# Layer 0's values: half of the columns by seven block products instead of eight, with raw weights kept in the scores' memory, and the instruction order set by a written table of rank changes

## The chip, the cores and the metric

The program runs on one core of a Trainium2 chip. The metric is device time in microseconds of one execution. Five engines matter: TensorE (PE in the profile; its weight loads are PEld), VectorE (DVE), ScalarE (ACT), GpSimd (POOL) and SyncE (SP), which here only issues DMA transfers.

## The reference, cut to what matters

A two-layer encoder over 512 tokens of width 1024, float32 throughout. Layer 0 mixes tokens with neighbourhood attention (16 heads of 64, an 8 x 64 grid of tokens, a window of 16 columns), layer 1 with three dilated windowed attentions that are merged. Each is followed by an output projection and a SwiGLU feed-forward of width 2816, with an RMS norm before and after.

```python
def neighbourhood_attention(x, w_qkv, w_o, rpb):
    qkv = (x @ w_qkv).reshape(b, rows, GRID_W, 3, N_HEADS, HEAD_DIM)
    ...                                   # scores + bias, masked softmax p, for each grid row
        return jnp.einsum('bhqrk,bhrkd->bhqd', p.astype(vr.dtype), vr)
    ...
    return o @ w_o

def reference(...):
    for layer in range(DEPTH):
        h = rms_norm(x, norm_mix_pre[layer])
        h = neighbourhood_attention(...) if layer % 2 == 0 else dilated_attention(...)
        x = x + rms_norm(h, norm_mix_post[layer])
        h = rms_norm(x, norm_ffn_pre[layer])
        x = x + rms_norm(swiglu(h, ...), norm_ffn_post[layer])
```

The change touches `x @ w_qkv` of layer 0 for the V columns 512 to 1023, and the order in which all instructions of the program are issued.

## The kernel before, in words

**Arithmetic.** A float32 product is done as three fast matmuls. `split` writes a high part h (ACT, L437) and a low part l = value - h (DVE, L438) of each operand, and `mm3` issues h·h, h·l, l·h (L449, L450, L451), each normally 128x256. Small products of the attentions use plain float32 matmuls that fill only half of the 128x128 array, two side by side: P·V of layer 0 (`window_pv`, L845), and in layer 1 the second scores (L1350) and P·V (L1419, L1425).

**Seven products.** The large weight products are cut into 2x2 blocks and done with seven block products instead of eight, with sums of blocks on both sides. For activations the sums are built once in the pre-norm (`operands`, transposes `tr_a` at L671, sums on POOL at L695 to L701). For weights, class `Seven` and its subclass `Values` do it: `p1`, `p2`, `sums`, `d1`, `s2`, `s4`, `sums2`, `s3`, `x2b`; POOL adds raw weight blocks (in `Values` L577, L579, L580, L585), ACT and DVE split the sums, the sinks combine the results. Layer 0's query and key columns (`qk_unit`, banks `pp_n`), both feed-forwards and layer 1 work so. Layer 0's values do not: `v_quarter` makes 256 columns at a time, with 8 x 4 x 3 = 96 matmuls of 128x256 (banks `vp_n`), four quarters in all (`vq`).

**Layer 0 in stages.** Pre-norm, four quarters of V, then for each of eight pairs of heads: the pair's query and key unit, the scores `s` (L794, L795, L805, L806), maximum on DVE (`tensor_tensor_reduce`, profile lines L813, L817), exponent on ACT (L820), scaling by the reciprocal on ACT (L1213) and POOL (L1215), transposes `ta`, `tb` (L827 to L834), P·V `o` (L845). Then the output projection `yo`, residual and norm (`tr_o`), gate and up (`gu`), down (`yd`). Layer 1 goes on with `vp_d`/`vd`, `pp_d`, `sa`, `sb`, `t`, `o`, `yo`, and its feed-forward. Raw weights arrive by SP's queue (L433, `load2`) in a ring of two buffers, `raw`.

**Order.** Code order does not set what an engine does next. Class `Order` collects all instructions with their dependences, plans them with a list scheduler (`run`: among the ready instructions of an engine, lowest rank first) and fixes the resulting order of each engine's queue (`pin`). Every engine is in-order afterwards: a waiting instruction holds everything behind it. Before, `pin` makes 20 orders by planning forward and backward in turn, rates each by `usual` (three runs of a noisy model, `through`), takes the best and then tries, for each 100 us piece, the ranks of the others.

Of the kernel before, what the change touches and what calls it, by code (L numbers as in the profile page):

```python
# [78 lines left out]
def _cost(i, e):  # L79
# [49 lines left out]
    return 100, 100, False, 0, 0  # L129


class Order:
# [150 lines left out]
    def through(self, order, costs):  # L283

        left, ready, at, last = [len(p) for p in self.pred], [0.0] * len(self.all), [0] * 5, 0.0
        free, locked, half, kind, pipe = [0.0] * 5, [0.0] * 5, [0.0] * 2, 0, 0.0
        rest = [e for e in range(5) if order[e]]
        while rest:
            now, e, k = min((max(free[e], ready[order[e][at[e]]]), e, order[e][at[e]]) for e in rest
                            if not left[order[e][at[e]]])  # L290
            taken, later, lock, mode, size = costs[k]
            s = max(now, pipe - AHEAD) if e == 4 else max(now, locked[5 - e]) if lock else now
            if e == 0:
                if mode > 2:
                    s = max(s + SWITCH.get((kind, 3), 0), half[mode - 3])
                    half[mode - 3] = s + later - 200
                else:
                    s = max(s + SWITCH.get((kind, mode), 0), max(half) + 95)
                    taken += 100 * (kind == 3)
                kind = min(mode, 3)  # L300
            if lock:
                locked[e] = s + taken
            if size:
                pipe = max(s + taken, pipe) + size / RATE
                end = pipe + LANDING + later
            else:
                end = s + later
            free[e], last = s + taken, max(last, end)
            for v in self.succ[k]:
                same = self.engine[v] == e and not size  # L310
                ready[v] = max(ready[v], s + taken if same and e == 0 else end if same else end + SYNC)
                left[v] -= 1
            at[e] += 1
            if at[e] == len(order[e]):
                rest.remove(e)
        return last

    def usual(self, order):

        ends = []  # L320
        for seed in range(3):
            r, costs = random.Random(seed), []
            for e, (taken, later, lock, mode, size) in zip(self.engine, self.costs):
                if size:
                    later = r.gauss(300, 700) if size < 4e5 else r.gauss(50, 800)
                    later *= 1.6 if e == 3 else 1
                else:
                    later += r.expovariate(1 / 15)
                costs.append((taken, later, lock, mode, size))
            ends.append(self.through(order, costs))  # L330
        return sum(ends) / len(ends)

    def pin(self, tc, times, span):
        rank, found = list(range(len(self.all))), []

        self.costs = [(t, LATE if 0 < size < 2e4 else later, lock, mode, size) for t, later, lock, mode, size in self.costs]
        for _ in range(times):
            starts, order, end = self.run(rank, False)
            found.append((self.usual(order), end, rank, starts, order))
            starts, _, end = self.run([-s - c[1] for s, c in zip(starts, self.costs)], True)  # L340
            rank = [end - s - c[0] for s, c in zip(starts, self.costs)]
        found.sort(key=lambda f: f[0])

        best, end, rank, base, order = found[0]
        for lo in np.arange(0.0, max(base), span):
            part = [k for k, s in enumerate(base) if lo <= s < lo + span]
            for _, _, other, _, _ in found[1:13]:
                mixed, shift = list(rank), float(np.median([rank[k] - other[k] for k in part]))
                for k in part:
                    mixed[k] = other[k] + shift  # L350
                _, new, e = self.run(mixed, False)
                usual = self.usual(new) if e < end + 3000 else best
                if usual < best:
                    best, end, rank, order = usual, e, mixed, new
        for q in order:
            for m, n in zip(q, q[1:]):
                tc.add_manual_dep(self.all[n], self.all[m].name,
                                  mybir.DependencyInfo(mybir.DependencyClass.NoSync, mybir.DependencyReason.DATA),
                                  reason="order")
# [3 lines left out]
def encoder_kernel(ctx: ExitStack, tc: tile.TileContext, a: dict, out: bass.AP):  # L363
# [20 lines left out]
    def bank(use, name):  # L384
        return tagged(psum, [P, 512], F32, use, name, BANKS[use])
# [701 lines left out]
    def hl(mem, i, n):  # L1087
        return mem[:, i * D:i * D + n], mem[:, i * D + n:i * D + 2 * n]
# [81 lines left out]
    def whole(v):  # L1170
# [12 lines left out]
                    raw0 if qd == 0 else None) for qd in range(4)]  # L1183
# [8 lines left out]

    for j in range(PAIRS):
# [323 lines left out]
    order.pin(tc, 20, 1e5)  # L1517
# [82 lines left out]
```

## Time and profile before

| what | value |
|---|---|
| median of 3 runs | 1460.94 us (1460.33 to 1461.76) |
| profiled execution | 1460.49 us, of which the span is 1458.7 us |
| PE busy | 1423.1 us (98%), 10788 matmul records |
| DVE, ACT, POOL busy | 1179.3 us (81%), 902.1 us (62%), 541.0 us (37%) |
| mean granted TensorE clock | 0.997 |
| chain that ended last | PE 82%, DVE 7%, ACT 5%, issue 2%, DMA 1%, POOL 1% |

The span is the profiled stretch; the execution's own time lies 1.8 us above it. A plain float32 matmul shows as two records, since it runs in two passes; that is why the trace has about 400 more matmuls than the program. In the timeline, records of one line that follow each other are shown as one row with a count (x8).

### The profile page before, as it was taken

To read this page: it belongs to the slowest core of one execution; us is meant where nothing else is said; L and a number is where in the kernel's file an instruction comes from. 1 tells how busy PE (TensorE), PEld (TensorE's weight loads), DVE (VectorE), ACT (ScalarE), POOL (GpSimd) and SP (SyncE) were. 2 spreads that over 40 slices of the span, in tenths; PEclk is the share of its full clock that TensorE was granted. 3 is DMA by queue.
4 is the path that set the end of the run, shared out by engine and by line. 5 is a ranking of instruction groups with operands and counts; after the bars stand their busy time and mean duration, and the time that the engine had idled before them with its cause. 6 is when DMAs were issued, how large, how long until landed. Compare 5 with 4: busy or idle time off the path is not lost.

```text
span 1458.7 us, 27918 instructions
## 1 busy us (share of the span) xinstructions
PE 1423.1 (98%) x10788; PEld 1318.6 (90%) x10788; DVE 1179.3 (81%) x1876; ACT 902.1 (62%) x1819; POOL 541.0 (37%) x398
## 2 busy tenths in 40 slices
PE   7999999999999999999999999999999999999997
PEld 6998877999999888999999999999877999999886
DVE  5499976899999888878678678787667989998877
ACT  4478873655555657544477677887775645555664
POOL 5345524544430001765553433344213644340001
PEclk9999999999999999999999999999999999999999
DMA  5356578788234674445433343343675788944662
GB/s 204 125 196 166 186 249 215 257 240 219 99 117 142 198 231 164 156 154 173 131 105 102 111 139 95 97 146 117 218 222 201 212 213 259 269 151 152 200 218 95
DMA packets 86645, 253.22 MB, mean 174 GB/s; under 512 B 19312, under 2 KB 31600, under 8 KB 84464
## 3 DMA queue, kind: packets, MB, share of 16 engines
q1 hardware_dynamic: 77696, 197.69, 41.0%
q0 software_dynamic: 8672, 53.48, 14.3%
q8 instruction: 85, 1.39, 0.4%
q14 instruction: 48, 0.39, 0.1%
q10 hardware_dynamic: 144, 0.26, 0.0%
HBM read 229.24 MB, written 68.29 MB: 204 GB/s over the span
## 4 chain that ended last, share of the span: by engine, by line
PE 82%; DVE 7%; ACT 5%; issue 2%; DMA 1%; POOL 1%; SPq 0%; POOLq 0%; DVEq 0%; ACTq 0%
PE gu L449 9%; PE gu L450 9%; PE gu L451 9%; PE pp_d L449 4%; PE pp_d L450 4%; PE pp_d L451 4%; PE yd_s L451 3%; PE yd_s L449 3%; PE yd_s L450 3%; PE vd L449 2%; PE vd L450 2%; PE vd L451 2%; PE yd_pp L451 2%; PE yd_pp L449 2%; PE yd_pp L450 2%
## 5 line engine op out<-in xcount | busy, mean ns | idle before, releaser
L657 POOL TENSOR_TENSOR rs_yd<-v_yd,mhalf 128x1 f32<-128x1 f32 x8 | 13.2, 1654 | 259.0 <-DVE v_yd L655 259.0
L450 PE MATMUL gu<-rxc,h_a 128*128 128x256 f32 x352 | 98.9, 281 | 1.3 <-DVE rxc L674 1.3
L449 PE MATMUL gu<-rxc,h_a 128*128 128x256 f32 x352 | 98.4, 280 | 1.0 <-ACT h_a L437 0.7
L449 PE MATMUL gu<-rxa,h_c 128*128 128x256 f32 x352 | 98.6, 280 | 0.6 <-DVE mem L915 0.4
L451 PE MATMUL gu<-rxc,l_a 128*128 128x256 f32 x352 | 98.6, 280 | 0.1
L449 PE MATMUL gu<-rxa,h_b 128*128 128x256 f32 x352 | 97.9, 278 | 0.1
L451 PE MATMUL gu<-rxa,l_b 128*128 128x256 f32 x352 | 97.7, 278 | 0.2 <-DVE l_b L438 0.2
L450 PE MATMUL gu<-rxa,h_b 128*128 128x256 f32 x352 | 97.8, 278 | 0.0
L450 PE MATMUL gu<-rxa,h_c 128*128 128x256 f32 x352 | 97.6, 278 | 0.0
L451 PE MATMUL gu<-rxa,l_c 128*128 128x256 f32 x352 | 97.4, 278 | 0.0
L517 POOL TENSOR_TENSOR r_d<-r_d 128x512 f32<-128x512 f32 x24 | 35.2, 1465 | 163.3 <-DVE l_ad L438 131.3
L437 ACT ACTIVATE rxc<-mem 128x512 fp32r<-128x512 f32 (+2 forms) x90 | 55.7, 623 | 60.7 <-PE yd_pp L450 32.0
L517 POOL TENSOR_TENSOR r_gu<-r_gu 128x512 f32<-128x512 f32 x20 | 33.3, 1666 | 153.0 <-DVE l_a L438 79.4
L438 DVE TENSOR_TENSOR rxc<-mem,rxc 128x512 fp32r<-128x512 f32 (+2 forms) x90 | 64.9, 727 | 16.8 <-ACT rxc L437 16.6
L517 POOL TENSOR_TENSOR raw<-raw 128x512 f32<-128x512 f32 x24 | 40.7, 1696 | 76.2 <-DVE l_a L438 73.5
L450 PEld LDWEIGHTS gu<-rxc,h_a 128*128 128x128 f32 x352 | 66.9, 190 | 1.7 <-DVE rxc L674 1.7
L449 PEld LDWEIGHTS gu<-rxc,h_a 128*128 128x128 f32 x352 | 66.8, 190 | 1.5 <-ACT h_a L437 1.0
L449 PEld LDWEIGHTS gu<-rxa,h_c 128*128 128x128 f32 x352 | 66.2, 188 | 1.6 <-DVE mem L915 0.6
L451 PEld LDWEIGHTS gu<-rxc,l_a 128*128 128x128 f32 x352 | 66.8, 190 | 0.3 <-DVE l_a L438 0.3
L449 PEld LDWEIGHTS gu<-rxa,h_b 128*128 128x128 f32 x352 | 66.3, 188 | 0.4 <-ACT h_b L437 0.3
L451 PEld LDWEIGHTS gu<-rxa,l_b 128*128 128x128 f32 x352 | 66.2, 188 | 0.4 <-DVE l_b L438 0.4
L450 PEld LDWEIGHTS gu<-rxa,h_b 128*128 128x128 f32 x352 | 66.2, 188 | 0.3 <-DVE rxa L674 0.2
(609 smaller groups left out, 6114.2 us busy)
## 6 DMA issues: line engine op xcount, KB each, us to landing
wsum<-wd POOLq DMA_DIRECT2D x24, 1408.0 KB, 11.9
r_d<-dil_qk SPq DMA_DIRECT2D x48, 512.0 KB, 4.0
raw<-wg SPq DMA_DIRECT2D x24, 512.0 KB, 5.0
raw<-wu SPq DMA_DIRECT2D x24, 512.0 KB, 7.0
wsum<-wsum POOLq DMA_DIRECT2D x8, 1408.0 KB, 10.5
raw<-wsum SPq DMA_DIRECT2D x22, 512.0 KB, 4.3
r_gu<-wg SPq DMA_DIRECT2D x20, 512.0 KB, 4.8
r_gu<-wu SPq DMA_DIRECT2D x20, 512.0 KB, 5.6
```

What stands on the lines that cost most here:

```text
L437: act.activation(h, src, AF.Copy)
L438: dve.tensor_sub(l, src, h.bitcast(F32))
L449: i = pe.matmul(o, s[0], m[0], start=start, stop=False, skip_group_check=True)
L450: pe.matmul(o, s[0], m[1], start=False, stop=False, skip_group_check=True)
L451: pe.matmul(o, s[1], m[0], start=False, stop=stop, skip_group_check=True)
L517: self.added = e[0].tensor_add(q[0], q[0], q[2])
L657: pool.tensor_tensor(r, v, mhalf, op=ALU.pow)
```

## The change: what it does

**V.** Quarters 0 and 1 stay as they were. Quarters 2 and 3 become one `v_unit` named `nv` with the seven products, 7 x 24 = 168 matmuls of 128x256 instead of 2 x 96 = 192. Its raw weights do not use the ring `raw`: they lie in `ap[1152:3200]` and `ap[3712:5760]`, where the score buffers `p_` and `pt_` live later and where the pre-norm's buffers (`ea`) lived before; the kept product `p5` lies between them at `ap[3200:3712]`. The unit runs ahead of the loop over pairs. Over the whole program PE has 24 instructions less, POOL 4 more (the sums of raw weights, 128x1024 each), DVE 6 more and ACT 3 more. The number of transfers stays.

**Order.** `through`, `usual` and the mixing are gone. `pin` still makes the 20 orders, takes the one numbered `FIRST`, changes its ranks by a table of 83 rows (each takes a range of instructions, of one engine or of all, and shifts their rank or takes it from another of the 20), and plans once.

```diff
+FIRST, TABLE = 11, (
+    (2, 0, 1975, 2245, 0, -1223), (1, 0, 1147819, 1157014, 0, -82769), (0, 5, 867142, 884029, 18, -5379),
...
-    def through(self, order, costs):
...
-    def usual(self, order):
...
-    def pin(self, tc, times, span):
+    def pin(self, tc, times, first, table):
...
-            starts, order, end = self.run(rank, False)
-            found.append((self.usual(order), end, rank, starts, order))
-            starts, _, end = self.run([-s - c[1] for s, c in zip(starts, self.costs)], True)
+            starts, _, end = self.run(rank, False)
+            found.append((rank, starts))
+            starts, _, _ = self.run([-s - c[1] for s, c in zip(starts, self.costs)], True)
             rank = [end - s - c[0] for s, c in zip(starts, self.costs)]
-        found.sort(key=lambda f: f[0])
...
+        rank, base = list(found[first][0]), found[first][1]
+        for what, e, lo, hi, turn, by in table:
+            for k, s in enumerate(base):
+                if e in (5, self.engine[k]) and lo <= (k if what == 2 else s) < hi:
+                    rank[k] = by + (found[turn][0][k] if what == 0 else rank[k])
+        order = self.run(rank, False)[1]
...
     vq = [v_quarter(apv[:, qd * D:(qd + 1) * D], a["na_v"][qd], f"n{qd}",
-                    raw0 if qd == 0 else None) for qd in range(4)]
+                    raw0 if qd == 0 else None) for qd in range(2)]
+    vu = v_unit([load2(a["na_v"][qd], f"n{qd}", ap[:, r:r + 2 * D]) for qd, r in ((2, 1152), (3, 3712))], [bank("pp", f"vn{i}") for i in range(2)], xm,
+                apv[:, 2 * D:], "nv", ap[:, 3200:3712],
+                cycle([hl(rxc[:, 24:], 0, D), hl(rxs, 2, D), (vmem, ao[:, :D])]), lambda qd, half, o: None)
+    vq += [apv[:, qd * D:(qd + 1) * D].rearrange("p (t c) -> p t c", t=NT) for qd in (2, 3)]
...
+    run(vu, unit_of(0), unit_of(0))
     for j in range(PAIRS):
         run(unit_of(j), unit_of(j + 1), unit_of(j + 1))
```

`Values.sums` and `sums2`, which the unit calls, are these (q[0], q[1] are the two raw halves of quarter 2, q[2], q[3] those of quarter 3):

```python
            self.w22 = split(*next(self.slots), q[3])
            pool.tensor_add(q[0], q[0], q[2])
            self.w12 = split(*next(self.slots), q[0])
            pool.tensor_add(q[2], q[2], q[3])
            pool.tensor_add(q[3], q[0], q[3])
            self.w21 = split(*next(self.slots), q[3])
            ...
            pool.tensor_add(q[1], q[3], q[1])
```

Lines move: up to the inserted lines a line of the kernel before carries a number lower by 22 (L433 is L411, L449 is L427, L517 is L495, L671 is L649), after them lower by 17 (L1350 is L1333, L1419 is L1402, L1425 is L1408).

**Where it shows in the order: V's second half.** On SP's queue, before, the raw weights of quarters 2 and 3 (`r_n_480`, `r_n_591`) and behind them the first query and key weights (`na_qk`):

```order
L433 DMA r_n_369<-na_v 128x1024 x2
L433 DMA r_n_480<-na_v 128x1024 x2
L1205 DMA mem<-na_bias 128x384 x3
L433 DMA r_n_591<-na_v 128x1024 x2
L433 DMA r_n_702<-na_qk 128x1024 x2
L433 DMA r_n_706<-na_qk 128x1024 x2
```

And now, with the same two quarters going to `mem`:

```order
L411 DMA r_n_369<-na_v 128x1024 x2
L411 DMA mem<-na_v 128x1024
L411 DMA r_n_486<-na_qk 128x1024 x2
L411 DMA r_n_743<-na_qk 128x1024
L1188 DMA mem<-na_bias 128x384 x3
L411 DMA mem<-na_v 128x1024
L411 DMA r_n_743<-na_qk 128x1024
L411 DMA mem<-na_v 128x1024 x2
```

Two query and key buffers are now asked for ahead of the last raw weights of V. Those last three loads write where the pre-norm's `hs` buffers lie, and so wait for the last transposes of tokens, which stand on PE, before, among the first query and key unit:

```order
L450 MATMUL pp_n_709<-rxa,h_an_775 128x256
L451 MATMUL pp_n_709<-rxa,l_an_776 128x256
L671 MATMUL tr_a_3_218<-ident,mem 128x128 x4
L671 MATMUL tr_a_4_226<-ident,mem 128x128 x4
L449 MATMUL pp_n_709<-rxa,h_an_775 128x256
```

and now some 300 rows earlier, among V's quarters 0 and 1:

```order
L427 MATMUL vp_n_1_319<-h_n_0_261,rxa 128x256
L649 MATMUL tr_a_3_218<-ident,mem 128x128 x4
L649 MATMUL tr_a_4_226<-ident,mem 128x128 x4
L428 MATMUL vp_n_1_319<-l_n_0_262,rxa 128x256
L429 MATMUL vp_n_1_319<-h_n_0_261,rxa 128x256
```

**On POOL, at the same place.** Before, the first sums of raw query and key weights follow the pre-norm's sums at once:

```order
L699 TENSOR_TENSOR mem<-mem 128x512
L701 TENSOR_TENSOR mem<-mem 128x512
L517 TENSOR_TENSOR r_n_702<-r_n_702 128x512
L518 TENSOR_TENSOR r_n_702<-r_n_702 128x512
L949 DMA wsum_87<-wd 128x2816
```

Now the four wide sums of the V unit stand between:

```order
L677 TENSOR_TENSOR mem<-mem 128x512
L679 TENSOR_TENSOR mem<-mem 128x512
L555 TENSOR_TENSOR mem<-mem 128x1024
L557 TENSOR_TENSOR mem<-mem 128x1024
L558 TENSOR_TENSOR mem<-mem 128x1024
L563 TENSOR_TENSOR mem<-mem 128x1024
L495 TENSOR_TENSOR r_n_486<-r_n_486 128x512
```

**On PE in layer 1**, where the first P·V (`o_0`) meets the second scores (`sb`). Before, the two alternate, and each uses the array in another layout:

```order
L1419 MATMUL o_0_8415<-mem 64x256 x5
L1419 MATMUL o_0_8415<-mem 64x128 x4
L1425 MATMUL o_0_8415<-mem 64x4x32 x2
L1350 MATMUL sb_0_0_8737<-mem 128x128
L1350 MATMUL sb_1_0_8738<-mem 128x128 x3
L1425 MATMUL o_0_8415<-mem 64x4x32 x2
L1350 MATMUL sb_1_0_8738<-mem 128x128
L1350 MATMUL sb_0_0_8737<-mem 128x128
L1425 MATMUL o_0_8415<-mem 64x4x32 x2
L1350 MATMUL sb_0_0_8737<-mem 128x128
L1425 MATMUL o_0_8415<-mem 64x4x32
L1350 MATMUL sb_0_0_8737<-mem 128x128
```

Now the eight second scores stand together, alternating between the two halves of the array, and the P·V follows in one piece:

```order
L1333 MATMUL sb_0_0_8722<-mem 128x128
L1333 MATMUL sb_1_0_8723<-mem 128x128
L1333 MATMUL sb_0_0_8722<-mem 128x128
L1333 MATMUL sb_1_0_8723<-mem 128x128
L1333 MATMUL sb_0_0_8722<-mem 128x128
L1333 MATMUL sb_1_0_8723<-mem 128x128
L1333 MATMUL sb_0_0_8722<-mem 128x128
L1333 MATMUL sb_1_0_8723<-mem 128x128
L1402 MATMUL o_0_8400<-mem 64x256 x6
L1402 MATMUL o_0_8400<-mem 64x128 x4
L1408 MATMUL o_0_8400<-mem 64x4x32
L427 MATMUL pp_d_8591<-rxb_6275,h_cd_8809 128x256
```

Over the whole list of PE, a group (an unbroken run of half-array matmuls of one layout: L845, L1350, L1419, L1425) occurs 89 times before and 68 times now (layer 0: 20 and 17; layer 1: 69 and 51). Within a group the two halves of the array work side by side, so its longer half counts: added up over all groups, the columns of the longer half are 39744 before and 38464 now (layer 0: 8640 and 8384; layer 1: 31104 and 30080).

More of the change, by code (lines that the diff above doesn't have):

```diff
@@ L1 @@
 import heapq
-import random
 from contextlib import ExitStack, contextmanager
@@ L129, in _cost @@
     return 100, 100, False, 0, 0
+FIRST, TABLE = 11, (
[28 rows of a table added]
+)
 class Order:
@@ L281, in run @@
         return starts, order, max(s + max(c[1], c[4] and LANDING + c[4] / RATE) for s, c in zip(starts, self.costs))
-    def through(self, order, costs):
[L285 to L316, printed above, removed]
@@ L318, in usual @@
-    def usual(self, order):
[L320 to L331, printed above, removed]
@@ L1516, in encoder_kernel @@
     order.link(tags, places, extra)
-    order.pin(tc, 20, 1e5)
+    order.pin(tc, 20, FIRST, TABLE)
 def _blocks(w, cols):
```

11 lines of the change are left out of this document (removed), and 27 rows, old and new, of the table c.

## The prediction

> **What bounds the kernel now.** I read the page's totals and the chain that ended last, then the busy time of each engine by stage, then what PE waits for, and last the timeline of PE for prices.
>
> ```profile
> span 1458.7 us, 27918 instructions
> PE 1423.1 (98%) x10788; PEld 1318.6 (90%) x10788; DVE 1179.3 (81%) x1876; ACT 902.1 (62%) x1819; POOL 541.0 (37%) x398
> PE 82%; DVE 7%; ACT 5%; issue 2%; DMA 1%; POOL 1%; SPq 0%; POOLq 0%; DVEq 0%; ACTq 0%
> ```
>
> PE is busy for 1423.1 of 1458.7 us and holds 82% of the chain, so it is the bound, and 35.6 us are left in which it does nothing. Where these lie is seen by stage (stretch, its length, then busy time of PE, PEld, DVE, ACT, POOL, granted clock, DMA share, GB/s):
>
> ```profile
> 0.00:24.00 24.00, 13.76 (x89) 12.98 (x90) 15.22 (x19) 13.41 (x20) 11.55 (x18) 1.00 0.69 242
> 24.00:80.00 56.00, 55.91 (x472) 55.10 (x471) 25.98 (x30) 23.37 (x35) 20.91 (x16) 1.00 0.41 138
> 80.00:100.00 20.00, 18.36 (x153) 17.73 (x152) 19.01 (x38) 13.90 (x31) 11.60 (x12) 1.00 0.56 195
> 100.00:180.00 80.00, 79.92 (x618) 70.35 (x617) 75.28 (x190) 68.62 (x169) 45.27 (x46) 1.00 0.61 171
> 180.00:240.00 60.00, 57.90 (x322) 45.00 (x321) 40.39 (x94) 37.82 (x91) 19.11 (x26) 1.00 0.80 251
> 600.00:700.00 100.00, 100.00 (x852) 100.00 (x851) 82.19 (x56) 48.94 (x62) 65.01 (x26) 1.00 0.49 159
> 800.00:1050.00 250.00, 249.25 (x2160) 230.37 (x2157) 187.07 (x430) 188.03 (x493) 96.05 (x67) 1.00 0.41 125
> 1450.00:1458.70 8.70, 0.58 (x3) 0.15 (x1) 3.52 (x6) 0.69 (x2) 2.00 (x2) 0.68 0.31 121
> ```
>
> Ten of the 35.6 us lie in the first stretch and eight in the last, and the change touches neither. Layer 0's V and the first query and key unit (24 to 80) keep PE full while DVE, ACT and POOL are less than half busy. In the attention of layer 0 (100 to 180) PE is full too, but DVE is at 75.28 of 80: there PE can be made shorter only so far. Layer 1's attention (800 to 1050) leaves PE 0.75 us idle, with DVE and ACT at three quarters. The waits that are left are small (what PE waited for: us in total, times, longest):
>
> ```profile
> PE yo L449 <- DVE mn L817: 1.2, 1, 1.2
> PE s L805 <- POOL rxc L1199: 0.7, 1, 0.7
> PE ta L830 <- POOL mem L1215: 0.6, 1, 0.6
> PE pp_n L449 <- ACT mem L529: 0.6, 1, 0.6
> ```
>
> So a microsecond taken from PE's work counts, unless something new makes PE wait.
>
> **The change part by part.** Prices first, from PE's timeline in layer 0's V and attention (start, duration, instruction; a pipelined matmul costs the distance to the next start):
>
> ```profile
> 18.22 0.28 PE L449 MATMUL vp_n<-h_n,rxa 128*128 128x256 f32 x1
> ...
> 30.00 0.28 PE L450 MATMUL vp_n<-l_n,rxa 128*128 128x256 f32 x1
> 30.12 0.93 PE L671 MATMUL tr_a<-ident,mem 128*128 128x128 f32 x7
> ...
> 104.55 0.28 PE L450 MATMUL pp_n<-rxb,h_cn 128*128 128x256 f32 x1
> 104.67 0.28 PE L451 MATMUL pp_n<-rxb,l_cn 128*128 128x256 f32 x1
> 104.88 0.54 PE L845 MATMUL o<-mem 128*64 128x192 f32 x2
> 105.35 0.27 PE L827 MATMUL ta<-ident,mem 64*128 64x64 f32 x1
> ...
> 109.53 0.28 PE L450 MATMUL pp_n<-rxb,h_bn 128*128 128x256 f32 x1
> 109.73 1.08 PE L845 MATMUL o<-mem 128*64 128x192 f32 x8
> 110.75 0.38 PE L451 MATMUL pp_n<-rxb,l_bn 128*128 128x256 f32 x1
> ```
>
> From 18.22 to 30.00 there are a hundred 128x256 matmuls, so one costs 0.118 us; a transpose costs (0.93 - 0.28) / 6 = 0.11. Before a group of half-array matmuls the distance is 0.21 (104.67 to 104.88) or 0.20, so entering costs 0.09 more. The group of one 192-column matmul (two records) lasts to 105.35, 0.47 us; the group of four (eight records), whose longer half has 512 columns, lasts 1.02. Two groups, two unknowns: (1.02 - 0.47) / 320 = 1.72 ns per column of the longer half, and 0.14 us for each group whatever its length.
>
> 1. *V, seven products.* 24 matmuls less: 24 x 0.118 = **-2.8 us** on PE, in the stretch where PE is full. What has to be ready in time: the raw weights, four POOL sums and six splits on ACT and DVE. ACT, DVE and POOL are below half busy there, so the added splits cost nothing while that slack lasts; the sums are the narrow place:
>
> ```profile
> 34.79 1.29 POOL L701 TENSOR_TENSOR mem<-mem 128x512 f32<-128x512 f32 x1
> 54.86 1.29 POOL L517 TENSOR_TENSOR r_n<-r_n 128x512 f32<-128x512 f32 x1 [18.78 <-DVE l_an L438]
> ...
> L579 POOL TENSOR_TENSOR mem<-mem 128x1024 f32<-128x1024 f32 x3 | 9.9, 3306 | 0.2
> ...
> L577 POOL TENSOR_TENSOR mem<-mem 128x1024 f32<-128x1024 f32 x3 | 7.2, 2409 | 2.8 <-DVE l_ad L438 2.8
> ...
> 38.56 1.06 ACT L437 ACTIVATE h_n<-r_n 128x1024 fp32r<-128x1024 f32 x1 [1.66 <-PE vp_n L451]
> ...
> r_n<-na_v SPq DMA_DIRECT2D x8, 512.0 KB, 5.6
> ```
>
> POOL idles 18.78 us after the pre-norm's sums, which is where its four wide sums go (2.4 to 3.3 us each, as layer 1's V units show). I count PE's rows of the new order at 0.118 (transposes 0.11) from where the two orders part. The last token transpose ends at about 36.0; the two raw halves of quarter 3 may load then and land at about 41.9 by the 5.6 us to landing; the first sum ends at 44.3, ACT's high part of it (1.06) at 45.5, and PE wants it at 47.7. The third sum ends between 49.1 and 50.3, its high part between 50.2 and 51.5, and PE wants it at 52.0. So the unit has 2.2 us to spare at one place and 0.5 to 1.8 at the other: nothing, or up to 1.5 us should the transfers come 2 to 3 us late. I take 0.4. Layer 1's V units, made the same way, leave PE 100.00 of 100 us busy.
>
> 2. *The raw ring and SP's queue.* The transfers are the same; query and key weights are now asked for ahead of V's last three loads, which wait for transposes that moved forward by some 35 us. If these three stand waiting on SP, only the query and key weights behind them wait, and two buffers of those have gone ahead. The first scores' PE position comes at about 83 us by the same count, against 86.2 for the old order, where the trace has it at 88.85: the difference of 2.7 is waits and layout changes, among them 0.7 for `s` and 0.6 for `pp_n`. I take these two waits as half gone, **-0.6**; bounds 0 and -1.3.
>
> 3. *Grouping of half-array matmuls.* 21 groups fewer: by 0.14 + 0.09 each -4.8 us, but where such a group stood between two others (as in the layer 1 place shown) entering may cost nothing more, by 0.14 alone -2.9. Both kinds went, so I take the middle, 0.18 each: **-3.8**. The longer half has 1280 columns less, because the halves are filled more evenly: 1280 x 1.72 ns = **-2.2**. By place: layer 0 3 x 0.18 + 256 x 1.72 ns = -1.0, layer 1 the other -5.0. What covers that in layer 1 is PE's full queue (249.25 of 250); DVE and ACT have 62 us to spare in that stretch.
>
> 4. *End of layer 0's attention.* `yo` came three rows behind the last score and waited 1.2 us for DVE's maximum; it now follows 23 rows behind. **-1.2**, bounds 0 and -1.2.
>
> 5. *Softmax.* Between a head's last score and its first transpose PE needs other work. Counted at the same prices the new order leaves less of it in eleven of sixteen heads: 14.3 to 8.8 us for head 8, 13.8 to 8.8 for head 9, 9.5 to 6.0 for head 12, 6.8 to 4.8 for the last. All cuts add up to 29 us. What it must cover is seen once undisturbed:
>
> ```profile
> 201.74 0.42 DVE L817 CUSTOM_DVE_ANT_0 mem<-s,mem 128x256 f32<-128x256 f32 x1
> ...
> 204.62 0.91 ACT L1213 ACTIVATE mem<-mem,rc 128x256 f32<-128x256 f32 x2 [0.35 <-DVE rc L1210]
> ```
>
> From the first wide maximum to the end of the scaling (205.53) it is 3.8 us, and about 4.5 with the hand-over at both ends. Cuts down to 8 us cost nothing then, unless DVE or ACT are behind; the last four heads are at the edge. I take **+1.5**; bounds 0 and +10 (a third of all cuts).
>
> 6. *Stalls before gate and up.* They stay, as the order there has the same shape:
>
> ```profile
> 254.67 0.65 PE L671 MATMUL tr_o<-ident,mem 128*128 128x128 f32 x4 [1.18 <-DVE rxc L674]
> ...
> 257.51 0.38 PE L449 MATMUL gu<-rxc,h_a 128*128 128x256 f32 x1 [0.75 <-ACT h_a L437]
> 258.67 0.58 PE L450 MATMUL gu<-rxc,h_a 128*128 128x256 f32 x1 [0.77 <-DVE rxc L674]
> ...
> 259.26 0.41 PE L449 MATMUL gu<-rxc,h_a 128*128 128x256 f32 x1
> 259.47 0.41 PE L450 MATMUL gu<-rxc,h_a 128*128 128x256 f32 x1
> ```
>
> After them the matmuls stand 0.21 us apart, for sixteen of them: half speed, 16 x 0.095 = 1.5 us. The bounds are 0 and -3 (stalls and slow spell gone) or +1.5 (a second such spell elsewhere); I take 0. The Trainium skill, "TensorE: Matmul & The Clock Gate" (Part 1 and its closing table), has the array fall to half clock after an idle window of about 3.4 us, and so asks for no gap above some 3 us. The trace differs: the longest single gap here is 1.18 us, and the speed fell after several in a row. By the page's rule a late V unit (1.5 us) would keep the clock; by the trace a cluster of small waits could cost 1.5 us more.
>
> Where other stretches get a new order, I expect small waits to come as often as go: **+1.0** for the many places I could not follow, bounds -2 and +4.
>
> Sum: -2.8 + 0.4 - 0.6 - 3.8 - 2.2 - 1.2 + 1.5 + 0 + 1.0 = -7.7 us. Against the profiled execution of 1460.49 (span 1458.7 and 1.8 around it) that is 1452.8; the median of the runs is 0.45 above it, so I predict 1453 us.
>
> **The rivals.**
> *Only V's part arrives (A).* Attention in layer 0 is held by DVE (75.28 of 80 us) and the shorter covers come back as waits, and small waits eat layer 1's grouping: point 5 at +5 to +7 in place of +1.5 gives 1456.5 to 1458.7. For it: DVE's load; against it: 4.5 us needed against 8 left in most heads.
> *Slower (B).* The same place at its worst: a chain that needs 9 us with DVE and ACT behind, so that more than 12 of the 29 us of cuts come back. Price +13 to +15 on point 5 makes +4 to +6, 1465 to 1467; it decides from a mean need of about 9 us per head. Against it: `ta` waited 0.6 us in all before, with covers of 6 to 10 in the last heads.
> *V unit late (C).* Raw weights land 4 us later than counted: PE waits 3 us in mid-unit, then the slow spell of 1.5: 1457.
> *No change (D).* PE's records shrink but its pace is set elsewhere: only where DVE, ACT or a DMA ends last, 18% of the chain by the page; 1460.5. Little speaks for it.
> *Better than the sum (E).* Entering counts in full (-1.0), the new waits of +2.9 stay away, the half-speed spell is gone (-1.5): 1447.6.
>
> **How the numbers follow.** The forecast has 0.50, E 0.17, A 0.17, C 0.05, D 0.05, B 0.06. The predicted time is that of the first, whose own range is 1449.5 to 1456; the range of 8 in 10 reaches to E's end and into A: 1447 to 1458.5. A change below 0.2% (2.9 us) is about what this measurement cannot tell from none. Faster than 1458.0 are the forecast, E, C and most of A: 0.85. Within are D and the rest of A, 0.09. Slower than 1463.9 is B: 0.06.
>
> **What the profile after would show.** PE with 24 matmul records less and busy some 8 to 10 us less; `vn` from about 42 us on without a wait above 1 us; the first `s` at 84 to 86 in place of 88.85; `yo` without its 1.2 us; 800 to 1050's work about 5 us shorter with PE still full. I am wrong if `ta`, `tr_o` or `sa` wait several microseconds more than before, if PE waits for POOL's wide sums, or if PE's busy time falls and the idle time grows by as much.

## The result, and the profile after

| | before | after |
|---|---|---|
| median | 1461.35 us (1460.33 to 1462.1, 4 runs) | 1447.82 us (1445.02 to 1451.69, 4 runs) |
| ratio | | 0.9909, interval 0.9887 to 0.993 |
| profiled execution (span) | 1460.49 (1458.7) | 1446.53 (1444.7) |

The change makes the kernel 13.5 us faster. Its runs spread over 6.7 us, those of before over 1.8 here; in the later sets, with more runs, those of before spread over 3 to 5.

The page's totals after:

```profile
span 1444.7 us, 27886 instructions
PE 1412.8 (98%) x10764; PEld 1315.0 (91%) x10764; DVE 1182.1 (82%) x1882; ACT 905.0 (63%) x1822; POOL 557.4 (39%) x402
```

PE has 24 matmuls less, as the V unit says, and is busy 10.3 us less; the span is 14.0 us shorter, so 3.7 us of idle time went too. By stage after (columns as in the table before; the first rows are of the same stretches):

```profile
24.00:80.00 56.00, 55.00 (x468) 54.64 (x468) 39.19 (x40) 29.10 (x43) 35.57 (x22) 1.00 0.40 138
80.00:100.00 20.00, 19.08 (x152) 17.65 (x151) 17.37 (x41) 13.82 (x33) 10.50 (x9) 1.00 0.38 135
180.00:240.00 60.00, 59.90 (x316) 46.47 (x316) 43.12 (x94) 35.80 (x88) 21.08 (x27) 1.00 0.79 244
240.00:262.00 22.00, 19.43 (x116) 17.41 (x115) 16.80 (x23) 11.83 (x22) 15.77 (x11) 0.84 0.91 274
```

DVE, ACT and POOL do more between 24 and 80 us (39.19, 29.10 and 35.57 for 25.98, 23.37 and 20.91) and PE is still full. From 180 to 240 PE idles 0.1 us, where it was 2.1. From 240 to 262, ahead of gate and up, the granted clock is 0.84, where it was 0.92 (1.00 is full speed; in a slow stretch the matmuls start 0.21 us apart in place of 0.12).

Where the 14.0 us of span came, in PE's timeline, by the first matmul of a stage:

| first matmul | before | after | difference | gain in the stage |
|---|---|---|---|---|
| scores `s`, layer 0 | 88.85 | 84.85 | -4.0 | 4.0 |
| `tr_o`, layer 0 | 252.46 | 246.03 | -6.4 | 2.4 |
| `vd` (layer 1's V units) | 612.44 | 607.49 | -4.9 | -1.5 |
| `tr_o`, layer 1 | 1119.83 | 1106.16 | -13.7 | 8.7 |
| last matmul | 1450.19 | 1436.17 | -14.0 | 0.4 |

So 8.7 of the 14 us come between layer 1's V units and its output projection, where only the order changed. The two rows for that stretch, before and after, as the stretch's length, then PE's busy time:

```profile
612.44:1119.83 507.39, 502.21 (x4127) 466.21 (x4126) 377.99 (x701) 336.99 (x792) 213.82 (x137) 1.00 0.44 140
```

```profile
607.49:1106.16 498.67, 494.37 (x4126) 463.58 (x4125) 377.50 (x701) 337.69 (x792) 213.54 (x137) 1.00 0.45 143
```

The same matmuls keep PE busy for 7.8 us less, and PE idles 4.3 us where it was 5.2. This stretch is used below to compare kernels: its length hardly depends on what happens elsewhere (498.67 here, 497.86 in the profile of experiment 1, the same kernel).

### The profile page after: what moved, and what is told of

The parts are those of the page before. It is cut to its first block, busy times and chain, and to the rows that moved or that the text cites. A ratio compares the mean times of both kernels' runs of the same rounds, so it can differ in the third digit from the quotient of the medians.

```text
span 1444.7 us, 27886 instructions
## 1 busy us (share of the span) xinstructions
PE 1412.8 (98%) x10764; PEld 1315.0 (91%) x10764; DVE 1182.1 (82%) x1882; ACT 905.0 (63%) x1822; POOL 557.4 (39%) x402
## 3 DMA queue, kind: packets, MB, share of 16 engines
q0 software_dynamic: 8672, 53.48, 14.4%
## 5 line engine op out<-in xcount | busy, mean ns | idle before, releaser
L635 POOL TENSOR_TENSOR rs_yd<-v_yd,mhalf 128x1 f32<-128x1 f32 x8 | 13.5, 1686 | 254.1 <-DVE v_yd L633 254.1
L427 PE MATMUL gu<-rxc,h_a 128*128 128x256 f32 x352 | 98.9, 283 | 1.4 <-ACT h_a L415 1.1
L427 PE MATMUL gu<-rxa,h_c 128*128 128x256 f32 x352 | 98.5, 280 | 0.1
L427 PE MATMUL gu<-rxa,h_b 128*128 128x256 f32 x352 | 97.8, 278 | 0.0
L495 POOL TENSOR_TENSOR r_d<-r_d 128x512 f32<-128x512 f32 x24 | 37.7, 1572 | 152.0 <-DVE l_ad L416 120.6
L416 DVE TENSOR_TENSOR rxc<-mem,rxc 128x512 fp32r<-128x512 f32 (+2 forms) x92 | 70.7, 776 | 20.6 <-ACT rxc L415 17.4
L495 POOL TENSOR_TENSOR r_gu<-r_gu 128x512 f32<-128x512 f32 x20 | 31.6, 1580 | 126.7 <-DVE l_a L416 69.8
L495 POOL TENSOR_TENSOR raw<-raw 128x512 f32<-128x512 f32 x24 | 40.3, 1682 | 91.6 <-DVE l_a L416 70.3
L427 PEld LDWEIGHTS gu<-rxc,h_a 128*128 128x128 f32 x352 | 67.0, 191 | 2.1 <-ACT h_a L415 1.3
L1297 ACT ACTIVATE mem<-mem 128x256 f32<-128x256 f32 x128 | 63.9, 503 | 7.7 <-DVE mem L1296 7.4
L427 PEld LDWEIGHTS gu<-rxa,h_c 128*128 128x128 f32 x352 | 66.2, 188 | 0.7 <-DVE mem L893 0.3
L428 PEld LDWEIGHTS gu<-rxa,h_b 128*128 128x128 f32 x352 | 66.2, 188 | 0.6 <-DVE rxa L652 0.6
```

Of the source, the lines that this page charges most:

```text
L416: dve.tensor_sub(l, src, h.bitcast(F32))
L427: i = pe.matmul(o, s[0], m[0], start=start, stop=False, skip_group_check=True)
L428: pe.matmul(o, s[0], m[1], start=False, stop=False, skip_group_check=True)
L495: self.added = e[0].tensor_add(q[0], q[0], q[2])
L635: pool.tensor_tensor(r, v, mhalf, op=ALU.pow)
L1297: act.activation(pr[:, f], pr[:, f], AF.Exp, bias=st[:, c:c + 1], scale=-1.0, accum_out=st[:, c + 2:c + 3])
```

## The experiments

In the kernels below, "the written sequence" means that `pin` gets the order of each queue as a list, not a plan:

```diff
-    order.pin(tc, 20, FIRST, TABLE)
+    order.pin(tc, PACKED)       # for each engine the instructions in sequence
```

The runs of before in these sets have a median of 1460.8 to 1461.9 us.

**1. The changed kernel again.** No edit.

> The changed kernel itself, once more. Its four runs so far lie between 1445.0 and 1451.7 us, while those of the kernel before lie within 1.8 us. If the clock's slow spell before gate and up decides (6.8 us at half clock in the profiled run), runs differ by up to 3.4 us and the profile of a longer or shorter run shows another slow spell; if the place is another, the times of the stages differ elsewhere. Expected 1448 us, spread of some 5 us.

Measured: 1447.21 us (1444.1 to 1450.72, 5 runs), 0.9908 (0.9893 to 0.9923). The profiled run of this set was the slowest, 1450.72. It has the same reduced clock before gate and up (0.84) and is level with the first profile up to layer 1's `tr_o` (1105.95 for 1106.16). The 4 us between them arise after that, in layer 1's feed-forward. That stretch in the first run and in this one:

```profile
1106.16:1436.20 330.04, 328.08 (x2372) 308.05 (x2370) 289.25 (x380) 190.97 (x321) 97.12 (x66) 1.00 0.67 200
```

```profile
1105.95:1439.94 333.99, 329.74 (x2372) 309.10 (x2370) 290.51 (x381) 191.28 (x321) 96.10 (x66) 1.00 0.66 197
```

Same matmuls, same clock of 1.00, 4 us apart: 1.7 of them PE busy time, 2.3 idle. Two waits of the longer run that the first has not make up 1.9 of the idle time:

```profile
PE tr_o L649 <- DVE rxa L652: 1.0, 2, 0.8
PE gu L427 <- ACT mem L507: 0.9, 1, 0.9
```

So the difference between these two is not the clock, and the kernel's nine runs say the same: the longest (1451.69) and the shortest (1444.1) both have a mean granted clock of 0.999.

**2. Layer 1 in the old order, and layer 0 in the old order.** Written sequences, joined at layer 1's first V matmul: (a) the changed kernel with layer 1's instructions in the sequence of before, (b) the kernel before with layer 1's in the new one.

> The changed kernel, with layer 1's instructions (from its first V matmul on) in the sequence they had before. Theory 1 (PE's work counts wherever it is taken away): layer 1's gain goes, 51 groups become 69 again and 1024 columns of the longer half come back, +5.0 us by the prediction's prices, +9 by the marks of the two traces (sa to the end); so about 1453 to 1457 us. Rival (the gain is in waits and the clock spell of layer 0, layer 1's order only moves waits about): no more than 2 us above the changed kernel.

> The kernel before, with layer 1's instructions in the new sequence; V with eight products and all of layer 0 as before. Theory 1: 1461 less 5 to 9 us, 1452 to 1456. Rival: 1459 to 1461. If the two halves add up, the gains of this one and of the one with layer 1 old sum to the whole 13.5 us.

Measured: (a) 1459.46 us (1457.06 to 1463.62, 12 runs), 0.9997 (0.9988 to 1.0007); (b) 1454.97 us (1452.48 to 1461.57, 12 runs), 0.9964 (0.9953 to 0.9976). The two gains are 1.4 us, which is not clear of noise, and 5.8, and they do not add up to 13.5. The stretch from `vd` to `tr_o`, (a) and then (b):

```profile
612.74:1121.36 508.62, 501.97 (x4126) 466.05 (x4125) 374.93 (x701) 337.01 (x792) 213.53 (x137) 1.00 0.44 140
```

```profile
614.15:1114.04 499.89, 495.44 (x4127) 464.09 (x4126) 379.14 (x701) 337.23 (x792) 214.01 (x137) 1.00 0.45 142
```

With the old sequence it takes 508.6 (before 507.4), with the new one 499.9 (after 498.7), whichever layer 0 stands ahead. Theory 1 holds for this stretch, and the rival falls: layer 1's order is worth 7.5 to 10 us. What (a) loses lies at the join, which neither kernel has by itself:

```profile
583.40 0.58 PE L489 MATMUL vp_d<-h_d,rxa 128*128 128x256 f32 x1 [3.70 <-ACT rxa L713]
583.78 0.41 PE L490 MATMUL vp_d<-l_d,rxa 128*128 128x256 f32 x1
...
589.07 0.41 PE L489 MATMUL vp_d<-h_d,rxa 128*128 128x256 f32 x1
589.28 0.35 PE L490 MATMUL vp_d<-l_d,rxa 128*128 128x256 f32 x1
```

PE waits 3.70 us and then runs at half speed (0.21 us apart) up to 589.3. Up to layer 0's `tr_o` (a) has kept its gain (246.99 for 252.46). In (b), layer 0 is that of before, yet the slow spell ahead of its gate and up is longer (granted clock 0.81 from 252.19 to 270 us, for 0.90 in the kernel before from 252.46), and `vd` starts 1.7 us later (614.15 for 612.44). The total of a joined kernel says little; its stretches do.

**3. Eight products in the scores' memory.** The V unit undone, the rest left:

```diff
-    vu = v_unit([load2(a["na_v"][qd], f"n{qd}", ap[:, r:r + 2 * D]) for qd, r in ((2, 1152), (3, 3712))], ...)
+    vq = [v_quarter(..., raw0 if qd == 0 else load2(a["na_v"][qd], f"n{qd}", ap[:, (0, 0, 1152, 3712)[qd]:][:, :2 * D])
+                    if qd > 1 else None) for qd in range(4)]
-    run(vu, unit_of(0), unit_of(0))
```

> The changed kernel with the second half of V by eight products again (24 matmuls more), its raw weights still in the scores' place, every other instruction in the new sequence. Theory 1: 24 x 0.118 = 2.8 us more than the changed kernel, about 1450.6. Rival (that stretch has slack elsewhere, since the scores wait for splits of query and key weights anyway): within 1 us of the changed kernel.

Measured: 1454.22 us (1452.21 to 1456.03, 5 runs), 0.9959 (0.9946 to 0.9972), 7 us above the changed kernel, where 2.8 was expected. The first score starts at 92.1 us for 84.85. Most of the excess is two waits that this order has, in which a split of query weights comes late, and a spell at half speed behind them, where the changed kernel has none:

```profile
80.26 0.39 PE L490 MATMUL pp_n<-rxa,h_an 128*128 128x256 f32 x1 [2.30 <-ACT h_an L478]
81.52 0.39 PE L492 MATMUL pp_n<-rxa,l_an 128*128 128x256 f32 x1 [0.76 <-DVE l_an L479]
```

```profile
80.00:100.00 20.00, 18.51 (x139) 17.89 (x140) 17.22 (x34) 13.21 (x28) 7.04 (x7) 0.91 0.39 136
```

So this run prices its order as much as the product, and fits neither of the two expectations.

**4. One product twice.** The clean form of the same question: 24 matmuls more and nothing else.

```diff
-            self.prod(self.left, split(*wslot(f"a{self.name}"), self.q[0]), X1A, True)
+            w = split(*wslot(f"a{self.name}"), self.q[0])
+            for _ in range(2 if self.name == "nv" else 1):
+                self.prod(self.left, w, X1A, True)
```

> The changed kernel, with the first of the seven products of layer 0's V unit done twice in a row: 24 matmuls more, no other instruction, no new dependence. Prediction: 24 x 0.118 = 2.8 us more. Rival (layer 0's scores wait for splits on DVE whatever PE does ahead of them): under 1 us. If it is 2.8, the 6.7 us that eight products cost in the run before are 2.8 us of work and 4 us of waits and clock made by that order.

Measured: 1454.72 us (1452.51 to 1454.82, 5 runs), 0.9949 (0.9937 to 0.9961). The first score starts 2.7 us later, and the later stages of layer 0 keep that (`tr_o` 248.76 for 246.03):

```profile
87.56 0.28 PE L848 MATMUL s<-rxc 128*128 128x256 f32 x1
```

```profile
84.85 0.28 PE L783 MATMUL s<-rxc 128*128 128x256 f32 x1
```

So 24 matmuls are worth 2.7 us there, as predicted, and the rival (under 1 us) falls. But the total rose by 7. In the profiled runs the last matmul comes 6.0 us later (1442.14 for 1436.17), and 3.7 of that arise in layer 1's feed-forward: it takes 333.70 us for 330.01, with a granted clock of 0.93 from 1100 to 1125 us for 1.00. The same stretch took 333.99 in experiment 1, where nothing was changed, so this part cannot be put down to the product. Experiment 7 takes this up.

**5. Groups cut in two.** In layer 1, 19 groups get the following full matmul into their middle:

```diff
 sb x16 records
-o  x20 and x2
-pp_d
+o  x8
+pp_d
+o  x12 and x2
```

> The changed kernel, with 19 groups of half-array matmuls of layer 1 cut in two: the 128x256 matmul that followed the group now stands in its middle. The columns of the longer halves stay as they are, so only the price of a group is measured. The prediction's 0.18 us each gives +3.4 us, its upper price of 0.23 gives +4.4, the lower of 0.14 gives +2.7; all of it in layer 1's attention. Rival (what layer 1's order brought was fewer waits, not fewer groups): less than 1 us.

Measured: 1456.93 us (1454.03 to 1460.87, 10 runs), 0.9966 (0.9955 to 0.9977). The stretch from `vd` to `tr_o`:

```profile
608.17:1114.51 506.34, 501.91 (x4127) 465.15 (x4125) 376.02 (x701) 337.75 (x792) 214.23 (x137) 1.00 0.44 141
```

It is 7.7 us longer than in the changed kernel, nearly all of it PE busy time (501.91 for 494.37): 0.40 us for a cut, above the prediction's highest price of 0.23. The rival (less than 1 us) falls. One place in the timeline, the changed kernel and then this one:

```profile
793.70 1.95 PE L1402 MATMUL o<-mem 128*64 128x256 f32 x20
795.49 0.38 PE L1408 MATMUL o<-mem 128*64 128x128 f32 x2
795.80 0.39 PE L427 MATMUL pp_d<-rxb,h_cd 128*128 128x256 f32 x1
```

```profile
795.05 1.08 PE L1466 MATMUL o<-mem 128*64 128x256 f32 x8
796.07 0.38 PE L491 MATMUL pp_d<-rxb,h_cd 128*128 128x256 f32 x1
796.38 1.09 PE L1466 MATMUL o<-mem 128*64 128x256 f32 x12
797.30 0.38 PE L1472 MATMUL o<-mem 128*64 128x128 f32 x2
797.61 0.39 PE L492 MATMUL pp_d<-rxb,h_cd 128*128 128x256 f32 x1
```

The group takes 795.80 - 793.70 = 2.10 us whole, and 797.61 - 795.05 = 2.56 cut. The matmul in the middle would cost 0.12 among its like, so the cut costs 0.34; that matmul alone takes 0.31 to the next start (796.07 to 796.38). All 19 do (0.312 to 0.318), where a full matmul that follows another one takes 0.206 at the median to the group behind it. So a group costs its 0.14 here too, but to enter one from a single full matmul costs 0.19 more and not 0.09; 19 x 0.34 = 6.5 of the 7.7 us. The Trainium skill, "TensorEngine Tiling (Array Packing)" (Tiling Modes, Key Properties), says that changing the tiling mode drains the TensorE; the trace shows a cost at such changes, 0.34 us for the cut here, and does not show what it consists of.

**6. Merging.** On the changed kernel, 32 first parts of groups moved later on PE's queue, to the rest of their group.

```diff
-o0_0 x1
 ... 74 rows of others
-o0_0 x7
+o0_0 x8
```

> The changed kernel, with 32 first parts of half-array groups moved later on PE's queue, directly ahead of the rest of the same group: 68 groups become 36, the columns of the longer halves 38464 become 35328. By the prediction's prices 32 x 0.18 + 3136 x 1.72 ns = 11.2 us less (9.9 to 12.8). Rival: the first parts stood where PE would else have waited, so less than half arrives, and PE's waits in the attentions grow by the rest.

Measured: 1481.63 us (1479.12 to 1483.3, 4 runs), 1.0136 (1.0123 to 1.015): 34 us slower than the changed kernel, where 11 faster was the prediction's price. The stretch from `vd` to `tr_o`, and what PE waits for in layer 1's attention:

```profile
608.87:1137.28 528.41, 495.53 (x4126) 465.71 (x4125) 375.54 (x701) 338.22 (x792) 210.55 (x137) 0.98 0.42 135
```

```profile
PE pp_d L489 <- ACT h_ad L477: 5.8, 3, 4.2
PE yo L489 <- ACT mem L805: 5.6, 1, 5.6
PE yo L490 <- DVE l_wo L478: 2.9, 1, 2.9
```

PE idles 32.9 us of it, for 4.3 after the change. Only PE's queue was moved: ACT's and DVE's stayed, so an instruction there that now waits longer for a late score or P·V holds what stands behind it, the splits of weights among them, and PE waits for those. The stretch also has half speed in three places, 17 us in all (granted clock 0.50 from 870.8 to 874.2 and from 1055.1 to 1065.3, 0.51 from 932.2 to 935.6), and PE's busy time did not fall. The rival holds: here, groups in one piece brought nothing while the other queues kept their order.

**7. The clock before gate and up.** Transposes of the identity (written to banks that are overwritten) in PE's waits: 20 ahead of layer 0's gate and up; then also 8 ahead of layer 1's; then that with the product done twice; then that with six first parts of `o` groups merged in layer 1, at most 30 rows away.

```diff
             b, g = bank(("s", "s", "pp", "o", "pp", "pp")[f % 6], f"gu{layer}_{f}"), next(g_)
+            for _ in range(((12, 8), (0, 8))[layer][f] if f < 2 else 0):     # the first kernel: layer 0 alone
+                pe.transpose(b[:, 0:P], ident, ident)
```

> The changed kernel, with 20 transposes of the identity more on PE, written to banks that the gate and up products overwrite: 12 in the wait between the two pairs of transposes ahead of gate and up, 8 in the wait behind them. If short waits in a row bring the half-clock spell there (6.8 us at half clock in the changed kernel, 3.4 in the kernel before), the spell goes and 1.7 to 3.4 us with it. Rival (the spell comes from something else, or the fill delays the products): no gain, or up to 1 us more.

> The changed kernel with the filled waits ahead of layer 0's gate and up, as before, and 8 transposes of the identity in the wait of 1.3 us ahead of layer 1's gate and up too, where the run with the first fill alone showed a half-clock spell of 3.4 us that the changed kernel's profiled run did not have. If clock spells are what the first fill's gain was lost to, and what spreads the changed kernel's runs over 6 us, no spell is left but the one at the end, the time is 1.5 to 3 us below the changed kernel, and the runs lie closer together. Rival (the pace of the last feed-forward varies by itself): the same time and the same spread.

> The kernel with both waits filled, and the V unit's first product done twice (24 matmuls more). Twice the product alone cost 2.8 us at the start of gate and up, but 7 us in all. If the other 4 came from clock spells that a shift of 2.8 us brings or takes away, it is now 2.8 us (2.5 to 3.3) above the kernel with both waits filled. Rival (the delay of the attention costs more farther on): again 5 to 8 us.

> The kernel with both waits filled, and six first parts of layer 1's P.V groups moved up to 30 rows later, to the rest of their group (51 groups become 45, 384 columns less); none of second scores, none in the last two pairs, none in layer 0. By the prediction's prices 6 x 0.18 + 384 x 1.72 ns = 1.7 us less; by the 0.4 us that a cut in the middle cost, 3 us less. Rival (as with 32 parts moved: what is moved later makes PE wait): no gain or a loss.

| kernel | median (range) | ratio to before |
|---|---|---|
| layer 0 filled | 1448.11 (1445.4 to 1449.87, 4 runs) | 0.9907 (0.9894 to 0.992) |
| both filled | 1444.97 (1443.79 to 1449.68, 5 runs) | 0.9900 (0.9886 to 0.9914) |
| both, product twice | 1450.34 (1446.86 to 1453.65, 6 runs) | 0.9927 (0.9913 to 0.9941) |
| both, six parts merged | 1453.08 (1451.88 to 1456.27, 5 runs) | 0.9950 (0.9938 to 0.9962) |

With the first fill the clock stays up ahead of layer 0's gate and up, and `vp_d` starts at 577.90 for 579.24. But the profile has a new slow stretch in layer 1, at a wait as long as the changed kernel's, which had none there. The first fill's rows for 240 to 262 and for 1100 to 1125, and the changed kernel's for the second stretch:

```profile
240.00:262.00 22.00, 21.65 (x157) 19.53 (x156) 16.98 (x24) 14.39 (x25) 15.66 (x11) 1.00 0.88 273
1100.00:1125.00 25.00, 23.45 (x163) 21.53 (x162) 20.53 (x30) 15.53 (x28) 18.32 (x14) 0.93 0.44 154
```

```profile
1100.00:1125.00 25.00, 23.45 (x167) 21.27 (x165) 21.25 (x29) 16.25 (x30) 17.08 (x13) 1.00 0.47 168
```

With both filled, the clock is 1.00 from 14.4 us to the end of the last matmul, and the median is 2.2 us below that of experiment 1; the intervals against before (0.9886 to 0.9914 and 0.9893 to 0.9923) overlap, so that it beats the changed kernel is likely and not shown. The range of its runs is still 5.9 us, with a mean granted clock of 0.998 or 0.999 in each: the rival holds, the spread comes from something else than the clock.

The product done twice costs 5.4 us here by the medians and 3.9 by the ratios, each of which is known to about 2 us, so the 2.8 of the prediction is not excluded. Its first score and `tr_o` come 3.0 us later, the last matmul of the profiled run 4.6. No slow stretch is left in either profile, so what there is beyond 3.0 is not a clock spell; it stays open. The six merged parts cost 8 us: fewer groups again, and more waits (PE waits 2.9 us for `h_ad` in three places, where it was 1.2 in one).

**8. The order without its table.**

```diff
-FIRST, TABLE = 11, ( ... 83 rows )
+FIRST, TABLE = 11, ()
```

> The changed kernel with the table of rank changes left empty: V by seven products, raw weights in the scores' place, and order number 11 of the 20 as it is. It has 88 groups in place of 68 and 1792 columns more in the longer halves: 20 x 0.18 + 1792 x 1.72 ns = 6.7 us above the changed kernel by the prediction's prices, so about 1454, if it waits no more than that. Rival (the table's worth is in waits, not in groups): more than 10 us above, with PE's idle time grown.

Measured: 1467.39 us (1465.25 to 1469.66, 5 runs), 1.0045 (1.0033 to 1.0057): 20 us above the changed kernel, and above the kernel before. The first score comes at 84.84 us, as with the table. The stretch from `vd` to `tr_o`, and its waits:

```profile
607.64:1119.47 511.83, 504.33 (x4131) 469.07 (x4130) 385.03 (x701) 337.74 (x793) 212.89 (x138) 1.00 0.44 139
```

```profile
PE pp_d L398 <- DVE pp_d L456: 2.1, 1, 2.1
PE tr_o L620 <- DVE rxc L623: 1.7, 2, 1.2
PE pp_d L398 <- DVE mem L709: 1.6, 2, 1.4
```

It is 13.2 us longer than with the table: 10.0 of it PE's busy time, 3.2 idle. Another 7 us come in layer 1's feed-forward (336.9 for 330.0), which has slow clock and waits there: the granted clock is 0.50 from 1124.3 to 1131.1 and 0.51 from 1216.4 to 1219.9, which is up to 5 of the 7. The expected 6.7 us is less than what the stretch's busy time alone grew by, and the rival (more than 10, with idle time grown) has the number: the table is worth groups, waits and slow spells together.

Up to `vd` this kernel is level with the changed one (607.64 for 607.49), but not because the table does nothing there. Layer 0's `tr_o` comes at 248.03 us for 246.03, and the 2 us are made good ahead of gate and up: nearly the same two waits as in the changed kernel (1.4 and 1.0 us, there 1.4 and 1.1) brought no slow spell here. The rows for 240 to 262 of this kernel and of two others with such waits, experiments 4 and 3:

```profile
240.00:262.00 22.00, 19.46 (x129) 17.09 (x128) 20.64 (x24) 12.52 (x23) 16.22 (x12) 1.00 0.92 294
240.00:262.00 22.00, 19.46 (x113) 16.93 (x111) 18.46 (x25) 10.32 (x19) 13.98 (x11) 0.92 0.98 287
240.00:262.00 22.00, 19.46 (x106) 16.11 (x105) 16.00 (x25) 9.81 (x20) 12.63 (x11) 1.00 1.02 276
```

V by seven products with the plain order number 11 loses 6 us against before, whose order had been picked and mixed from the 20.

## Why the prediction was right, and where its sizes were off

Forecast 1453 us (range 1447 to 1458.5), measured 1447.8. The direction and the mechanism held: PE's work counted wherever it was taken away. The size did not: the forecast's own range began at 1449.5, and the result lies in the wider one by 0.8 us, where rival E had its 1447.6. Of what E asked for, the new waits stayed away, but the slow spell before gate and up grew instead of going, so that its number came is partly luck. By the prediction's terms:

1. *V, seven products* (-2.8): 2.7 by experiment 4. The wait of 0.4 did not come. POOL's first wide sum ended 2.5 us ahead of the time counted, the third at 48.73, 0.4 us ahead of the early bound:

```profile
39.36 2.40 POOL L555 TENSOR_TENSOR mem<-mem 128x1024 f32<-128x1024 f32 x1 [8.36 <-DVE l_bnv L416]
41.84 2.42 POOL L557 TENSOR_TENSOR mem<-mem 128x1024 f32<-128x1024 f32 x1
45.51 3.22 POOL L558 TENSOR_TENSOR mem<-mem 128x1024 f32<-128x1024 f32 x1 [1.25 <-DVE rxc L416]
```

2. *Ring and queue* (-0.6): about 0. The first `s` no longer waits its 0.7 and `pp_n` still waits 0.5 for 0.6, but the query unit waited 1.0 us for DVE's clearing of a bank (L485), which the prediction did not have. The first score gained 4.0 us, more than terms 1 and 2. The array reached full clock at 14.7 us for 16.1, and the unbroken stream of V's matmuls behind it starts at 17.70 for 18.10, which is 0.4 of it; two matmuls of query and key units fewer stand ahead of the first score, 0.2; the rest is not told apart.

3. *Groups* (-6.0): this term was right in kind and near in size. In the stretch from `vd` to `tr_o` I sorted every distance from one matmul's start to the next by layout. Full to half: 56 distances, 11.90 us, became 42 and 9.44. Half to full: 56 and 13.26 became 42 and 9.13. Between `o` and `sb`: 13 and 2.62 became 9 and 1.82. Inside a group: 603 and 49.30 became 621 and 49.18. That is -7.5, and 14 more distances between full matmuls give 1.65 back: -5.9 for layer 1, predicted -5.0. Of the 18 groups fewer there, 14 stood between full matmuls and 4 between `o` and `sb`, so the upper price of 0.23 was right for most: 14 x 0.23 + 4 x 0.14 + 1.8 for the columns is 5.5. A cut in the middle costs more (0.34), because it leaves a single full matmul between two groups, and the change removed none of that kind.

   The prices themselves hold over all of layer 1. The 55 groups of `o` in both traces that have no wait last 0.147 us + 1.70 ns for each column of the longer half, to within 0.006 us (root mean square; the columns are from the kernels' instruction lists). A line through the columns of both halves misses by 0.087. Second scores are different: their order counts too. Eight of them with 512 columns in the longer half last 1.09 us where the halves alternate, as in the place shown ahead of the prediction, and 1.42 in the sequence abbbbaaa (a and b are the halves). The prediction's count of columns does not see this. Layer 0's -1.0 was not measured by itself.

4. *End of layer 0's attention* (-1.2): the wait of `yo` for DVE's maximum is gone from the list, and 180 to 240 is full.

5. *Softmax* (+1.5): this step failed too. It was 0: no wait of `ta` is left in the list of after; covers of 4.8 to 9 us were enough. This was the term that rivals A and B stood on, and neither came.

6. *Before gate and up* (0): the loss grew. The rows after:

```profile
248.48 1.26 PE L649 MATMUL tr_o<-ident,mem 128*128 128x128 f32 x8 [1.41 <-DVE rxc L652]
...
251.40 0.58 PE L427 MATMUL gu<-rxc,h_a 128*128 128x256 f32 x1 [1.08 <-ACT h_a L415]
251.78 0.42 PE L428 MATMUL gu<-rxc,h_a 128*128 128x256 f32 x1
...
255.84 0.41 PE L429 MATMUL gu<-rxc,l_a 128*128 128x256 f32 x1
```

The matmuls stand 0.21 apart from 251.78 to 255.84, twenty of them and four transposes behind. Before, thirteen stood so (259.05 to 261.82; the sixteen of the prediction is a miscount): about 1 us more. The fill of experiment 7 got 1.3 back. It is most of the -1.5 of the table's third row. With nearly the same two waits the spell stayed away in two other kernels (experiment 8), so the order does not settle the size of this term.

7. *Places not followed* (+1.0): this step failed. It was -2.8 in layer 1's attention (the 8.7 less the 5.9 of groups), as the wait ahead of `sa` (the row is of before; there is none in the list now) and long distances between transposes (4.6 us before, 2.4 now) went:

```profile
PE sa L1330 <- DVE mem L1313: 1.3, 1, 1.3
```

The prediction took gains and losses to balance, without a reason why they should. In the profiled runs the change is 14.0 us for a sum of 7.7. Terms 5 and 7 together, +2.5 predicted and about -2.8 measured, are 5.3 of the 6.3 between them; the rest is what is left of smaller misses, of which the loss before gate and up has the other sign.

## What to carry to other kernels

Where PE is full, price an order by its changes of layout: count the groups of half-array matmuls, the longer half of each and the single full matmuls between two groups, over the whole list. But experiment 6 shows the limit: the same count, brought down further by moving PE's queue alone, cost 34 us, while the queues of ACT and DVE kept their old order. And a difference of some 3 us in the total can be a slow spell that comes or stays away behind the same waits: look at the granted clock of both profiles first. When pieces of two orders are joined, compare them stretch by stretch; the seam can cost more than the piece is worth.

## What was not expected of the hardware

- The half-speed spell does not follow a wait by its length alone. A wait of 3.70 us brought one in experiment 2; waits of 1.41 and 1.08 us in close succession brought more than 4 us of it in the changed kernel (granted clock 0.84), less in experiment 4 (0.92), and none in experiments 3 and 8 (1.00), with waits of 1.41 and 1.05; and ahead of layer 1's gate and up, the same wait of 1.31 us brought one in the kernel with the first fill (granted clock 0.93 above, first row) and none in the changed kernel (1.00, second row):

```profile
1109.30 0.38 PE L492 MATMUL gu<-rxc,h_a 128*128 128x256 f32 x1 [1.31 <-DVE rxc L716]
```

```profile
1111.48 0.39 PE L428 MATMUL gu<-rxc,h_a 128*128 128x256 f32 x1 [1.31 <-DVE rxc L652]
```

  The Trainium skill, "TensorE: Matmul & The Clock Gate" (Part 1 and its closing table), describes a free-running window of about 3.4 us and asks for no gap above some 3 us. That the phase of such a window decides would fit these rows, and no run shows it; to keep every single gap below 3 us was not enough here, with 1.41 us as the longest.
- At a granted clock of 1.00 the same list of 128x256 matmuls ran at a median of 0.114 us in one stretch of a feed-forward and of 0.117 in another, and which stretch was which changed from run to run; the two rows of experiment 1, 328.08 and 329.74 us busy, are such a pair. What sets it was not found. With the waits beside it, it makes the 4 us between those two runs, out of a spread of 6 to 7.
